# The four column groups' products of the modulation and the square sums, ordered one right behind another

## Chip, core and metric

The kernel runs on one core of a Trainium2 chip. The metric is device time in microseconds of one execution; the times before are the median of three runs. Engines are named as in the profile: PE is TensorE's matmuls and PEld its weight loads, DVE is VectorE, ACT ScalarE, POOL GpSimdE, SP the engine whose queue issues most of the DMAs.

## The reference, cut to what matters

A two-layer backbone over 1024 latent tokens and 256 context tokens, model width 1024, all in fp32. For each layer the conditioning vectors of latent and context tokens give a shift, a scale and a gate of 1024 numbers each:

```
def modulation(cond, w, b):
    m = jax.nn.silu(cond) @ w + b
    return jnp.split(m, 3, axis=-1)

h_lat = rms_norm(x_lat, norm_g[i]) * (1.0 + sc_l[:, None, :]) + sh_l[:, None, :]
y_lat, y_ctx = even_mixer(...)   # i = 0: global and windowed attention, 8 heads each
y_lat, y_ctx = odd_mixer(...)    # i = 1: convolution branch and neighbourhood attention
x_lat = x_lat + g_l[:, None, :] * y_lat
```

The result is `rms_norm(x_lat, final_g)`. Each rms norm needs, for each token, the sum of 1024 squares.

## The kernel before

Activations lie transposed: 128 of the 1024 channels on the partitions, tokens along the free dimension, in pieces of 256, 512 and 512 tokens. Each projection is done as three matmuls of split numbers (`mm3`, L351 to L354), accumulated over eight channel blocks in one PSUM bank. Layer 0 weaves attention (scores L529 to L533, outputs L480 to L485, row maxima L643 to L663) with the projections (`pq` and `pg`) of the next head group; layer 1 does the same with its own projections and, later, the output projection (`po`).

Two small sums use TensorE differently. They have only few output rows, so they use a quarter of the array's columns each, and write to one of four groups of 32 partitions of the bank:

- The modulation (`mod_part`, L181). Half of one of the three vectors, 512 columns, is the sum of eight products: `csil`, the activated conditioning of one channel block, 32 columns wide, by a 128x512 block of `mod_w` (tiles `mw`, loaded by SP). Block `dk` goes to column group `dk % 4`, so that each group sums two blocks. There are 12 banks `pm` of eight products. The first four banks are made by `mod_half` (L204) at the start of the program, with two blocks to a load. The other eight are made by `mod_steps` (L215), with four blocks to a load, so two calls of `mod_part` to a bank. This generator is advanced by `tick` (L831), in the middle of projections. A copy on ScalarE (L234) and four matmuls with `msel` (`mod_out`, L187) then add the four groups up.
- The square sum (`sum4`, L282). Squares of four channel blocks, summed over partitions by a matmul with ones, one block to a column group. Four banks `pb` of two calls each: in the norm of layer 0 (`norm_x`), at the end of layer 0 (`final_proj(1)`), and twice in the final norm (`out1_end`, pieces 1 and 2). The matmul of the block computed last, `i = 3`, is recorded first, and the three others are held behind it by `tc.issue_after`.

The order on each engine is not the order of the code. The framework's scheduler lays the instructions out along a timeline of its own: among those that are ready it takes the one with the lower priority number, which is the place in the recording unless the kernel changes it. `later(n)` (L292) adds `n` to that number for what is recorded inside; `tick` uses `later(100)` for the modulation, so that its steps yield to the projections. `tc.issue_after(x)` keeps what is recorded inside behind instruction `x`. Each engine then runs its own list strictly in order, waiting on semaphores; SP's list is a queue of DMA issues, in which each load of a tile with a limited number of buffers waits until its buffer is free. Names with numbers, such as pm_1024, are single tiles of a family.

Of the kernel before, what the change touches and what calls it, by code (L numbers as in the profile page):

```python
# [89 lines left out]
def tile_kernel(ctx: ExitStack, tc: tile.TileContext, a, out):  # L90
    nc = tc.nc
    VE, SC, GP, PE, SY = nc.vector, nc.scalar, nc.gpsimd, nc.tensor, nc.sync
# [50 lines left out]
    csil = kvp.tile([P, DK, 32], F32, tag="csil", name="csil")  # L143
# [36 lines left out]

    def mod_part(pb, w, dks):  # L181

        for k, dk in enumerate(dks):
            q = dk % 4 * 32
            PE.matmul(pb[q : q + 32, :], csil[:, dk, :], w[:, k, :], start=(dk < 4), stop=(dk >= 4))

    def mod_out(tr, row, l, part, j):  # L187

# [15 lines left out]
    def mod_half(l, part, j):  # L204

        pb = bank("pp", nm("pm"))
        for d2 in range(4):
            w2 = mw_tile()
            mm0.append(SY.dma_start(w2, mod_src(l, part, j, 2 * d2, 2 * d2 + 2)))
            mod_part(pb, w2, (2 * d2, 2 * d2 + 1))  # L210
        row = a0.tile([P, 512], F32, tag="ost", name=nm("mrow"), bufs=2)
        SC.copy(row, pb)
        mod_out(bank("tr", nm("trm")), row, l, part, j)

    def mod_steps(pool, halves):  # L215

        def load(l, part, j):
            ws = []
            for d in (0, 4):
                w = pool.tile([P, 4, 512], F32, tag="mw", name=nm("mw"), bufs=2)  # L220
                SY.dma_start(w, mod_src(l, part, j, d, d + 4))
                ws.append(w)
            return ws

        ws = load(*halves[0])
        for n_, hf in enumerate(halves):
            for _ in range(4):
                yield
            tag = "ov" if solo[0] else "tr"
            pb = bank(tag, nm("pm"))  # L230
            for d, w in enumerate(ws):
                mod_part(pb, w, range(4 * d, 4 * d + 4))
            row = pool.tile([P, 640], F32, tag="rt2", name=nm("mrow"), bufs=2)[:, :512]
            SC.copy(row, pb)  # L234
            yield
            yield
            mod_out(bank("ov" if solo[0] else "tr", nm("trm")), row, *hf)
            if n_ + 1 < len(halves):
                ws = load(*halves[n_ + 1])
            for _ in range(3):  # L240
                yield
# [40 lines left out]
    def sum4(pb, sqs, n, q):  # L282

        with ExitStack() as cx:
            for i in (3, 0, 1, 2):
                m = PE.matmul(pb[32 * i : 32 * i + 32, :n], one[:, 0:1].broadcast_to([P, 32]), sqs[i][:, :n],
                              start=(q == 0), stop=(q == 1))
                if i == 3:
                    cx.enter_context(tc.issue_after(m.ins))

    @contextmanager
    def later(n):  # L292

        p = tc.cur_priority
        tc.cur_priority = p + n
        yield
        tc.cur_priority -= n
# [418 lines left out]
    with ExitStack() as p0x:  # L716
# [6 lines left out]
        with tc.tile_pool(name="st0", bufs=1, reuse_waits="tile") as st0:  # L723
# [19 lines left out]
            def norm_x(c):  # L743
                n = CHUNKS[c][1]
                if c == 1:
                    pb = bank("st", nm("pb"))
                    for q in range(2):
                        sqs = []
                        for i in range(4):
                            j = 4 * q + i  # L750
                            if j < 6:
                                sq = kvp.tile([P, 512], F32, tag=("QH", "QL")[j % 2], name=nm("sq"), bufs=3)
                            else:
                                sq = a0.tile([P, 512], F32, tag="ost", name=nm("sq"), bufs=2)
                            SC.activation(sq[:, :n], xraw[c][4 * q + i], AF.Square)
                            sqs.append(sq)
                        sum4(pb, sqs, n, q)
                    acc = kvp.tile([P, 512], F32, tag="QH", name=nm("acc"), bufs=3)
                    acts0.append(SC.copy(acc[:, :n], pb[:, :n]))
                    return acc  # L760
# [223 lines left out]
    with tc.tile_pool(name="o0", bufs=1, reuse_waits="tile") as op_:  # L984
# [49 lines left out]
        def final_proj(c):  # L1034
# [9 lines left out]
            for e in range(DK):  # L1044
                yield from out0(final, e, c, *ws[e // 2])
                if c > 0:
                    SY.dma_start(X1[:, e, t0 - 256 : t0 - 256 + n], x1[c][:, e, :])
                if c == 1:
                    sqs.append(op_.tile([P, 512], F32, tag="sq1" if e % 4 < 3 else "acc1", name=nm("sq1"), bufs=3 if e % 4 < 3 else 1))
                    SC.activation(sqs[-1], x1[c][:, e, :], AF.Square)  # L1050
                    if e == 0:
                        pb = bank("tr", nm("pb"))
                    if e % 4 == 3:
                        sum4(pb, sqs[-4:], n, e // 4)
                    if e == 7:
                        accs[c].append(acc1())
                        SC.copy(accs[c][0], pb)
                elif e < na:
                    SC.activation(accs[c][e], x1[c][:, e, :], AF.Square)
                else:  # L1060
                    if c < 2:
                        sq = op_.tile([P, 512], F32, tag="sq1", name=nm("sq1"), bufs=3)
                    else:
                        sq = kvp.tile([P, 512], F32, tag="QL", name=nm("sq1"), bufs=3)
                    SC.activation(sq[:, :n], x1[c][:, e, :], AF.Square)
                    k = e % na if e < 7 else 0
                    (GP if (k if c == 2 else e % 2) else VE).tensor_tensor(accs[c][k], accs[c][k], sq[:, :n], op=ALU.add)
# [44 lines left out]
    with ExitStack() as l1x:  # L1112
# [407 lines left out]
        def out1_end(k):  # L1520
# [4 lines left out]
            for e in range(DK):  # L1525
                if k == 0:
                    if e % 2 == 0:
                        w = load_w(wp, a["od_wo"], e // 2, 256, WB, dks=range(4, 8))
                    yield from out1((4, 5, 6, 7), e, hf, *w, o, n)
                else:  # L1530
                    yield from out1((7,), e, hf, *wend[e // 2], o, n)
                x = x2[hf][:, e, o : o + n]
                if k:
                    sq = dlow.tile([P, 512], F32, tag=("ph", "pl")[e % 2], name=nm("sq2"), bufs=LOOK1 + 1)[:, :n]
                else:
                    sq = half("sq2", "hf") if e in SQ else pair("sqt", 512, "vT")[:, 0].bitcast(F32)
                SC.activation(sq, x, AF.Square)
                if k:
                    accs.append(sq)
                    if e % 4 == 3:  # L1540
                        sum4(pb, accs[-4:], n, e // 4)
                elif e in SQ:
                    accs.append(sq)
                else:
                    (GP if e in SQP[k] else VE).tensor_tensor(accs[e % 2], accs[e % 2], sq, op=ALU.add)
                yield
# [188 lines left out]
```

## Time and profile before

| | us |
|---|---|
| median of 3 runs | 1530.31 (1528.89 to 1530.62) |
| span of the profiled execution, first to last instruction | 1528.5 |
| TensorE busy in it | 1451.0 |
| the modulation's products (L185), 192 records, PE busy | 43.8 |
| the square sums' products (L286), 64 records, PE busy | 8.3 (5.3 at 512 columns, 3.0 at 256) |

The profiled execution's own time is known by its span alone. Each fp32 product of the two sums shows as two records, each projection matmul as one. A matmul's length in the profile contains its run through the array, so consecutive ones overlap; what one costs TensorE is read from the distance of starts. Stretches are given in us from the span's start: the modulation and first norm up to about 36 us, layer 0's attention woven with projections to about 900, layer 1's convolution to about 1180, its attention to about 1500, then the final norm.

### The profile page before, as it was taken

Reading aid. Unit: us, or ns where it says so; the run is one execution under the profiler, and the core shown is the slowest. Engines: PE = TensorE matmul, PEld = TensorE weight load, DVE = VectorE, ACT = ScalarE, POOL = GpSimd, SP = SyncE. Lnnn points to the kernel's source line nnn. Section 1 sums busy time; section 2 is a strip of 40 time slices with the busy share of each in tenths; the row PEclk is TensorE's granted clock in tenths of the full one; section 3 lists DMA queues with packets and bytes.
Section 4 is the critical chain, followed back from the end, with each engine's and each line's share of the span. In section 5 each row is a group of like instructions: output and inputs, shape, how many; then the busy total and the mean of one; then the engine's idle time right before and its main releaser. Section 6 shows DMA issues by size and latency. Waiting matters only on the chain.

```text
span 1528.5 us, 21545 instructions
## 1 busy us (share of the span) xinstructions
PE 1451.0 (95%) x7144; PEld 1167.2 (76%) x7144; DVE 1031.7 (67%) x2095; ACT 748.1 (49%) x1418; POOL 788.0 (52%) x628
## 2 busy tenths in 40 slices
PE   6999999998998999999999889999999999989996
PEld 2786877896896777886777568888887788868775
DVE  2643566589578856457676948899848666567766
ACT  3642433443435564447646665343334455455564
POOL 3360443555454766557645665665532434364665
PEclk9999999999999999999999999999999999989998
DMA  9564325422312246121202021210484677877642
GB/s 366 201 225 135 106 69 174 135 77 88 114 56 76 85 138 210 49 69 54 59 28 66 35 67 56 62 56 28 158 253 144 207 219 240 248 222 234 178 129 110
DMA packets 154167, 199.83 MB, mean 131 GB/s; under 512 B 14716, under 2 KB 95816, under 8 KB 154056
## 3 DMA queue, kind: packets, MB, share of 16 engines
q1 hardware_dynamic: 147392, 186.88, 38.9%
q10 hardware_dynamic: 6664, 11.57, 2.3%
q8 instruction: 56, 0.92, 0.3%
q14 instruction: 55, 0.45, 0.1%
HBM read 148.07 MB, written 49.02 MB: 129 GB/s over the span
## 4 chain that ended last, share of the span: by engine, by line
PE 79%; DVE 11%; issue 3%; DMA 3%; ACT 2%; POOL 1%; ACTq 0%; SPq 0%; DVEq 0%; POOLq 0%
PE p L352 6%; PE p L354 6%; PE p L353 6%; PE ov L480 5%; PE ov L482 4%; PE ov L481 4%; PE po L352 4%; PE st L533 4%; PE st L529 4%; PE po L353 4%; PE po L354 4%; PE pq L352 4%; PE pq L353 3%; PE pq L354 3%; PE pg L352 2%
## 5 line engine op out<-in xcount | busy, mean ns | idle before, releaser
L334 POOL TENSOR_TENSOR pl<-pf,ph 128x512 fp32r<-128x512 f32 (+4 forms) x321 | 394.0, 1239 | 384.9 <-ACT ph L331 337.3
L541 ACT ACTIVATE pf<-st 128x512 f32<-128x512 f32 x284 | 166.5, 597 | 203.6 <-PE st L533 165.2
L334 POOL TENSOR_TENSOR wl<-wr,wh 128x512 fp32r<-128x512 f32 (+2 forms) x131 | 169.3, 1302 | 136.5 <-ACT wh L331 124.0
L331 ACT CAST ph<-pf 128x512 fp32r<-128x512 f32 (+4 forms) x364 | 209.5, 588 | 27.1 <-PE ov L481 15.9
L352 PE MATMUL p<-hh,wh 128*128 128x512 f32 x448 | 176.0, 393 | 3.4 <-DVE spq L1233 1.3
L353 PE MATMUL p<-hl,wh 128*128 128x512 f32 x448 | 174.5, 390 | 0.0
L354 PE MATMUL p<-hh,wl 128*128 128x512 f32 x448 | 173.0, 391 | 0.0
L480 PE MATMUL ov<-ph,Vt 128*128 128x512 f32 (+4 forms) x364 | 141.0, 387 | 4.2 <-DVE y L693 2.0
L529 PE MATMUL st<-QH,KAt 128*128 128x512 f32 (+4 forms) x364 | 140.2, 386 | 3.9 <-ACT pf L541 3.1
L482 PE MATMUL ov<-pl,Vt 128*128 128x512 f32 (+4 forms) x364 | 141.1, 388 | 2.2 <-POOL pl L334 2.1
L481 PE MATMUL ov<-ph,Vt 128*64 128x512 f32 (+4 forms) x364 | 138.9, 381 | 0.0
L533 PE MATMUL st<-QL,KBt 68*128 68x512 f32 (+4 forms) x364 | 136.4, 386 | 0.9 <-issue 0.8
L1177 DVE SCALAR_TENSOR_TENSOR cps<-U,taps,cps 128x512 f32<-128x512 f32 x184 | 125.9, 748 | 0.7
L331 ACT CAST wh<-wr 128x512 fp32r<-128x512 f32 (+2 forms) x134 | 80.9, 613 | 84.1 <-PE po L353 15.9
L352 PEld LDWEIGHTS p<-hh,wh 128*128 128x128 f32 x448 | 84.2, 188 | 21.5 <-ACT spq L1231 1.6
L656 DVE TENSOR_REDUCE mp<-mx 128x1 f32<-128x512 f32 x128 | 85.3, 681 | 19.3 <-PE mx L655 18.3
L354 PEld LDWEIGHTS p<-hh,wl 128*128 128x128 f32 x448 | 84.1, 188 | 17.4
L353 PEld LDWEIGHTS p<-hl,wh 128*128 128x128 f32 x448 | 84.2, 188 | 17.1 <-issue 0.2
L1020 DVE SCALAR_TENSOR_TENSOR x<-po,modT,x 128x512 f32<-128x512 f32 (+1 forms) x72 | 46.9, 657 | 64.0 <-PE po L354 63.5
L352 PE MATMUL pq<-wh,hh 128*128 128x384 f32 x256 | 88.2, 344 | 1.0 <-ACT hh L331 1.0
L353 PE MATMUL pq<-wl,hh 128*128 128x384 f32 x256 | 87.3, 341 | 0.0
L354 PE MATMUL pq<-wh,hl 128*128 128x384 f32 x256 | 86.6, 342 | 0.0
(287 smaller groups left out, 3417.2 us busy)
## 6 DMA issues: line engine op xcount, KB each, us to landing
mw<-in_mod_w_dram SPq DMA_DIRECT2D x16, 1024.0 KB, 5.3
Q<-qs SPq DMA_DIRECT2D x40, 256.0 KB, 2.1
QH<-Q SPq DMA_DIRECT2D x80, 128.0 KB, 2.7
mw<-in_mod_w_dram SPq DMA_DIRECT2D x16, 512.0 KB, 6.8
wr<-in_od_d_dram SPq DMA_DIRECT2D x32, 256.0 KB, 3.1
wr<-in_ev_qkv_dram SPq DMA_DIRECT2D x16, 384.0 KB, 5.0
KAt<-KD SPq DMA_DIRECT2D x16, 384.0 KB, 6.5
wr<-in_od_wo_dram SPq DMA_DIRECT2D x22, 256.0 KB, 3.4
```

The source lines that it names most:

```text
L331: acts.append(SC.copy(hi, src))
L334: (GP if leng == "g" else VE).tensor_tensor(lo, src, hi.bitcast(F32), op=ALU.subtract)
L352: PE.matmul(o, lh, rh, start=first, stop=False)
L353: PE.matmul(o, lh, rl, start=False, stop=False)
L354: last.append(PE.matmul(o, ll, rh, start=False, stop=end))
L480: PE.matmul(o, V[:, 64:192], ph[:, :n], start=(t == 0), stop=False)
L481: PE.matmul(g.ov[0:64, q0 : q0 + n], V[:, 0:64], ph[:, :n], start=False, stop=False)
L482: PE.matmul(o, V[:, 64:192], pl[:, :n], start=False, stop=(last and g.sink is None))
L529: sts.append(PE.matmul(st[:, :n], KA[:, cs], g.QH[:, q0 : q0 + n], start=True, stop=False))
L533: PE.matmul(st[:, :n], KB[0:68, cs], g.QL[0:68, q0 : q0 + n], start=False, stop=True)
L541: acts.append(SC.activation(pf[:, :n], st[:, :n], AF.Exp, scale=1.0 if g.bias else SCALE))
L1177: VE.scalar_tensor_tensor(pc, uc, w, pc, op0=ALU.mult, op1=ALU.add)
```

## The change

```
@@ mod_part
-        for k, dk in enumerate(dks):
-            q = dk % 4 * 32
-            PE.matmul(pb[q : q + 32, :], csil[:, dk, :], w[:, k, :], start=(dk < 4), stop=(dk >= 4))
+        with ExitStack() as cx:
+            for k, dk in enumerate(dks):
+                q = dk % 4 * 32
+                m = PE.matmul(pb[q : q + 32, :], csil[:, dk, :], w[:, k, :], start=(dk < 4), stop=(dk >= 4))
+                if k == 0:
+                    cx.enter_context(tc.issue_after(m.ins))
+                    cx.enter_context(later(-100000))
@@ sum4
         with ExitStack() as cx:
             for i in (3, 0, 1, 2):
+                if i == 0:
+                    cx.enter_context(later(-100000))
                 m = PE.matmul(pb[32 * i : 32 * i + 32, :n], one[:, 0:1].broadcast_to([P, 32]), sqs[i][:, :n],
                               start=(q == 0), stop=(q == 1))
```

The first product of a call keeps its place in the schedule. The others of the call are held behind it and get a priority number that is lower than any other's, so that the scheduler takes them as soon as they are ready. No instruction is added or removed on any engine. The new lines shift line numbers: L185 becomes L186, L286 becomes L292, and the lines behind move down by 4 (between the two places) or 6.

The first place at which the order differs is TensorE's list in the middle of a gate projection of layer 0 (pg_1127; products of bank pm_1024), about 112 us into the span. Before, from one projection matmul to the next:

```order
L352 MATMUL pg_1127<-hh_174,gh_996 128x512
L185 MATMUL pm_1024<-mw_908,csil 32x512
L353 MATMUL pg_1127<-hl_175,gh_996 128x512
L185 MATMUL pm_1024<-mw_908,csil 32x512
L354 MATMUL pg_1127<-hh_174,gl_997 128x512
L185 MATMUL pm_1024<-mw_908,csil 32x512
L352 MATMUL pg_1127<-hh_174,gh_996 128x512
L185 MATMUL pm_1024<-mw_908,csil 32x512
L932 MATMUL trk_1058<-ident,pc_803 128x128 x3
L353 MATMUL pg_1127<-hl_175,gh_996 128x512
L185 MATMUL pm_1024<-mw_910,csil 32x512
```

Of the change, the same place:

```order
L358 MATMUL pg_1127<-hh_174,gh_996 128x512
L186 MATMUL pm_1024<-mw_908,csil 32x512 x4
L359 MATMUL pg_1127<-hl_175,gh_996 128x512
L360 MATMUL pg_1127<-hh_174,gl_997 128x512
L358 MATMUL pg_1127<-hh_174,gh_996 128x512
L938 MATMUL trk_1058<-ident,pc_803 128x128 x3
L359 MATMUL pg_1127<-hl_175,gh_996 128x512
L186 MATMUL pm_1024<-mw_910,csil 32x512 x4
```

The eight products, each between two projection matmuls, became two groups of four; the rest kept its order. Banks pm_2020 (four and four single ones), pm_3143 (five, two, one) and pm_3959 (one, seven) become two groups of four, one of eight and one of eight in the same way, and the square sum of `final_proj(1)` (one, three, four) two of four. The other modulation banks stood in groups already. Behind pm_2020 the scheduler's timeline runs differently, and instructions of all engines swap places with neighbours, in three stretches: up to about 480 us, about 840 to 960 us, and about 1200 to 1440 us.

The second place is SP's queue in layer 1's attention, where the keys (KAt), queries (QH, QL) and bias tiles (bm, bs) of a coming head are loaded, with weights (wr), about 1340 us into the span. Before:

```order
L1372 DMA bm_13525<-in_d_bm_dram 128x320
L371 DMA wr_14391<-in_od_wo_dram 128x512
L1382 DMA bs_13775<-in_d_bs_dram 128x320
L409 DMA KAt_11673<-KD_9582 64x1536
L410 DMA KAt_11673<-KD_9582 64x1536
L1361 DMA QH_13741<-QD_9578 64x512
L1362 DMA QH_13741<-QD_9578 64x512
L1363 DMA QL_13742<-QD_9578 64x512
L1372 DMA bm_13769<-in_d_bm_dram 128x440
```

Of the change:

```order
L377 DMA wr_14391<-in_od_wo_dram 128x512
L1388 DMA bs_13775<-in_d_bs_dram 128x320
L1378 DMA bm_13769<-in_d_bm_dram 128x440
L415 DMA KAt_11673<-KD_9582 64x1536
L416 DMA KAt_11673<-KD_9582 64x1536
L1367 DMA QH_13741<-QD_9578 64x512
L1368 DMA QH_13741<-QD_9578 64x512
L1369 DMA QL_13742<-QD_9578 64x512
```

The bias load bm_13769 moved from behind the keys and queries to ahead of them. At the head before it, the bias load bm_13274 moved the other way, from ahead of KAt_11670 to behind QL_13219.

The third place is the end of TensorE's list, with the last square sum (pb_15683), the transposing matmuls of the piece before it (trs_15672) and the broadcasts (bc). Before:

```order
L354 MATMUL po_3828_15737<-od_3247_13697,wl_15601 128x256
L267 MATMUL trs_15672<-ones,row_15670 128x2 x2
L286 MATMUL pb_15683<-sq_3821_15710,one 32x256
L286 MATMUL pb_15683<-sq_3815_15689,one 32x256
L286 MATMUL pb_15683<-sq_3817_15696,one 32x256
L286 MATMUL pb_15683<-sq_3819_15703,one 32x256
L286 MATMUL pb_15683<-sq_3829_15742,one 32x256
```

Of the change:

```order
L360 MATMUL po_3828_15737<-od_3247_13697,wl_15601 128x256
L292 MATMUL pb_15683<-sq_3821_15710,one 32x256
L292 MATMUL pb_15683<-sq_3815_15689,one 32x256
L292 MATMUL pb_15683<-sq_3817_15696,one 32x256
L292 MATMUL pb_15683<-sq_3819_15703,one 32x256
L271 MATMUL trs_15672<-ones,row_15670 128x2 x2
L292 MATMUL pb_15683<-sq_3829_15742,one 32x256
```

The first four products moved ahead of the transposing matmuls.

## The prediction

> **What bounds the kernel now.** I read the page from the top: the span, the engine totals, the granted clock, then who ends the chain.
>
> ```profile
> span 1528.5 us, 21545 instructions
> PE 1451.0 (95%) x7144; PEld 1167.2 (76%) x7144; DVE 1031.7 (67%) x2095; ACT 748.1 (49%) x1418; POOL 788.0 (52%) x628
> PEclk9999999999999999999999999999999999989998
> PE 79%; DVE 11%; issue 3%; DMA 3%; ACT 2%; POOL 1%; ACTq 0%; SPq 0%; DVEq 0%; POOLq 0%
> ```
>
> TensorE is busy for 95% of the span, the chain that ended last runs over it for 79%, and its clock is granted in full nearly everywhere. So a microsecond taken out of its queue is worth up to a microsecond, as long as nothing else is late. Next, the stretches in which the change moves instructions:
>
> ```profile
> core 0: us, PE busy (x) PEld busy (x) DVE busy (x) ACT busy (x) POOL busy (x), PEclk, DMA share, GB/s
> 120.00:160.00 40.00, 38.84 (x203) 29.36 (x203) 15.64 (x48) 10.72 (x24) 5.12 (x4) 1.00 0.50 172
> 200.00:330.00 130.00, 128.63 (x672) 105.86 (x671) 80.87 (x204) 52.40 (x114) 56.73 (x43) 1.00 0.37 119
> 330.00:500.00 170.00, 161.64 (x816) 135.07 (x815) 133.83 (x302) 74.22 (x156) 86.81 (x63) 0.97 0.26 82
> 840.00:960.00 120.00, 108.57 (x479) 80.61 (x478) 87.21 (x155) 74.43 (x139) 72.56 (x70) 0.93 0.17 57
> 1200.00:1440.00 240.00, 231.91 (x1174) 192.52 (x1175) 159.44 (x379) 130.68 (x257) 116.31 (x107) 0.98 0.78 226
> ```
>
> From 120 to 160 and from 200 to 330 us TensorE has next to no idle time, while VectorE, ScalarE and GpSimdE have a third to four fifths of theirs free: TensorE alone is the bound. From 330 to 500 VectorE is at 133.83 of 170 us (79%), from 840 to 960 TensorE loses 11 us to waits, from 1200 to 1440 the DMA engines are at 78%. In these three a saving may be partly eaten.
>
> **What one product costs alone.** The timeline of TensorE where one bank's eight modulation products stand one by one among a gate projection (a projection matmul is one record, a product two; columns are start, length, then the instruction):
>
> ```profile
> 112.02 0.39 PE L354 MATMUL pg<-hh,gl 128*128 128x512 f32 x1
> 112.25 0.39 PE L352 MATMUL pg<-hh,gh 128*128 128x512 f32 x1
> 112.57 1.05 PE L185 MATMUL pm<-mw,csil 128*32 128x512 f32 x2
> 113.55 0.49 PE L353 MATMUL pg<-hl,gh 128*128 128x512 f32 x1
> 113.97 1.05 PE L185 MATMUL pm<-mw,csil 128*32 128x512 f32 x2
> 114.95 0.49 PE L354 MATMUL pg<-hh,gl 128*128 128x512 f32 x1
> ```
>
> Projections follow each other every 0.23 us (112.02 to 112.25). With one product between them it is 1.40 (113.55 to 114.95). So a product alone costs 1.40 - 0.23 = 1.17 us.
>
> **What a run costs.** First four products side by side, then eight:
>
> ```profile
> 68.02 0.34 PE L353 MATMUL pq<-wl,hh 128*128 128x384 f32 x1
> 68.29 1.06 PE L185 MATMUL pm<-mw,csil 128*32 128x512 f32 x8
> 69.29 0.44 PE L354 MATMUL pq<-wh,hl 128*128 128x384 f32 x1
> 69.57 0.49 PE L932 MATMUL trk<-ident,pc 128*128 128x128 f32 x3
> ...
> 143.91 0.40 PE L354 MATMUL pg<-hh,gl 128*128 128x512 f32 x1
> 144.23 1.92 PE L185 MATMUL pm<-mw,csil 128*32 128x512 f32 x16
> 146.09 0.44 PE L663 MATMUL mx<-KAt,QH 128*128 128x384 f32 x1
> 146.37 0.27 PE L457 MATMUL trn<-ident,nmt 128*12 128x128 f32 x1
> ```
>
> Four: 69.57 - 68.02 = 1.55 for the run and two 384-wide matmuls. Such a one is shorter than the 512-wide one's 0.23; at the ratio of their widths 0.17 (an estimate), which leaves 1.55 - 0.34 = 1.21 us. The four column groups together take what one takes alone: 1.06 against 1.05 in length. Eight: 2.46 - 0.23 - 0.17 = 2.06 us. So what counts is how often TensorE is interrupted, not how many products there are.
>
> On this the Trainium skill speaks against the change. The weight loads of the products, min, median and longest in ns:
>
> ```profile
> L185 PEld LDWEIGHTS pm<-mw,csil x192: 106/109/156, 8.6 to 356.2; 128*32 128x32 f32 x192
> ```
>
> Its page "TensorE: Matmul & The Clock Gate", Part 3, "The mechanism", says that a weight load overlaps a running matmul only where the row groups differ, and all four products here use all rows. By that rule, three further pairs of weight loads at the median of 109 ns would make a run of four 0.65 us dearer (6 x 0.109), some 1.86. The trace disagrees: 1.06 for four. I keep the row.
>
> **The change part by part.** The order shows that the instructions are the same; on every engine only their places change. Of the sixteen banks summed this way ten keep the shape they had, most because the scheduler already had them in fours or eights, or because modulation loads come two products at a time in the first 40 us. Six change.
>
> (1) Bank pm_1024, near 112 us: eight interruptions become two runs of four. 8 x 1.17 - 2 x 1.21 = **6.9 us**. Until here nothing else on any engine is moved, and after it TensorE stays the bound (38.84 of 40 us), with DMA at half share: kept in full.
>
> (2) Bank pm_2020 and (3) bank pm_3143, near 211 and 275 us:
>
> ```profile
> 211.41 1.07 PE L185 MATMUL pm<-mw,csil 128*32 128x512 f32 x8
> 212.78 1.05 PE L185 MATMUL pm<-mw,csil 128*32 128x512 f32 x2
> ...
> 275.16 1.90 PE L185 MATMUL pm<-mw,csil 128*32 128x512 f32 x10
> 278.06 1.05 PE L185 MATMUL pm<-mw,csil 128*32 128x512 f32 x4
> 279.42 1.05 PE L185 MATMUL pm<-mw,csil 128*32 128x512 f32 x2
> ```
>
> pm_2020 is a run of four and four single ones (the first shown): 1.21 + 4 x 1.17 = 5.9, afterwards two runs of four, 2.4: **3.5 us**. pm_3143 is runs of five, two and one. A run of five lasts as long as eight (1.90 against 1.92), one of two as long as one: 2.06 + 1.21 + 1.17 = 4.4, afterwards one run of eight, 2.06: **2.4 us**. Both lie where TensorE is 99% busy.
>
> (4) Bank pm_3959, near 351 us, a single one and seven, becomes eight: 1.17 us of TensorE time.
>
> ```profile
> 351.58 1.02 PE L185 MATMUL pm<-mw,csil 128*32 128x512 f32 x2 [0.86 <-issue]
> 354.71 0.28 PE L457 MATMUL trn<-ident,nmt 128*12 128x128 f32 x1 [1.32 <-DVE nmt L446]
> ```
>
> TensorE waits before it and 3 us later for VectorE, so the time freed is likely to become longer waiting. Between 0 and 1.17 I take **0**.
>
> (5) The square sum near 841 us: one, three, four becomes four, four.
>
> ```profile
> 841.31 1.04 PE L286 MATMUL pb<-sq,one 128*32 128x512 f32 x2
> 843.19 1.06 PE L286 MATMUL pb<-sq,one 128*32 128x512 f32 x6
> ```
>
> Lengths as above, so one interruption of 1.17 goes. In the stretch that follows TensorE waits a tenth of its time for others. Half of it: **0.6 us**, bounds 0 and 1.17.
>
> (6) The last square sum is split: four of its products now stand ahead of the transposing matmuls of the piece before it, with which the final norm's chain begins.
>
> ```profile
> 1515.47 0.50 PE L267 MATMUL trs<-ones,row 128*128 128x2 f32 x4
> 1515.90 1.83 PE L286 MATMUL pb<-sq,one 128*32 128x256 f32 x16
> ```
>
> Its cost lies between nothing and half of 1.83 us, since the products can hide the wait for their last squares; it is near the tail, nothing covers it: **-0.5 us**.
>
> (7) The new order elsewhere: 600-odd rows of TensorE in the stretches 211 to 480, 840 to 960 and 1200 to 1440 us swap places with neighbours, and with them loads on SP's queue. The dearest wait in the last of these stretches, and one issue on the queue ahead of it:
>
> ```profile
> 1350.82 0.77 PE L1405 MATMUL mx<-KAt,QH 128*128 128x256 f32 x2 [2.56 <-DMA QH<-QD]
> ...
> 1339.69 0.46 SPq L1372 DMA_DIRECT2D bm<-in_d_bm_dram  x1
> ...
> 1340.00:1350.00 10.00, 7.31 (x30) 4.93 (x28) 4.29 (x12) 6.80 (x15) 6.66 (x6) 0.84 1.04 280
> 1350.00:1360.00 10.00, 9.18 (x31) 7.58 (x32) 8.28 (x17) 3.95 (x9) 6.85 (x7) 0.66 0.71 182
> ```
>
> The order moves one bias load ahead of the KAt and QH loads of just this wait: QH is issued 0.46 us later if the bias tile's buffer is free, **-0.5 us**. A whole wait like this costs 2.56 us and, by the granted clock, 1.6 and 3.4 us of pace in the two tens: 7.6 us. For the other swaps the trace has no price; bounds are one such wait gained or lost, and I take 0, since neighbours trade places in both directions.
>
> Sum: 6.9 + 3.5 + 2.4 + 0 + 0.6 - 0.5 - 0.5 = **12.4 us**. The profiled execution's span of 1528.5 would become 1516.1. The median, 1530.31, lies 1.8 above that span; I carry this over: **1517.9 us**.
>
> **The rivals.** *One wait more or less.* The swaps add one wait of 7.6 us in the three stretches (1525.5), or dissolve the one at 1350 (1510.3). For it: DMA is at 78% to 104% there, and a queue in order delays all behind it. Against more than one: the instructions and bytes are the same.
>
> *Absorbed by VectorE.* If VectorE set the pace from 330 to 500 us, terms 1 to 3 would end as waiting there, and about nothing stay: 1530.7. Against it: VectorE has 36 us free in this stretch, three times the gain, and its work arrives earlier by as much.
>
> *Slower, by SP's queue in the last stretch.* Bias loads that now stand ahead of KAt and QH wait for a buffer, and hold these back at several head changes. Two such waits more give 1533.1, three give 1540.7; it decides from the second on, 15.2 against 12.4. Against it: the other reordered KAt group near it has its bias load moved behind QH instead.
>
> *Loads in line.* If the six loads that follow in a run of four took their 109 ns each, one after another, a run would cost 0.65 us more. Terms 1 and 2 end with four such runs where one stood: 3 x 0.65 = 2.0 us less, 1519.9. The 1.06 us of the run of four speaks against it. The Trainium skill's rule above would give this.
>
> **How the numbers follow.** My forecast has 54%, a wait dissolved 16%, a wait more 14%, loads in line 1%: faster in all of these, 85%. Absorbed 5% and two waits more 5% are within 0.2%, about 3 us and about what a measurement of this kernel can tell from no change: 10%. Three waits more: 5%, slower. The range takes in the forecast with its bounds (0 and 1.17 in terms 4 and 5) and a wait either way: 1508 to 1526.
>
> **What would show it.** Right: products as x8 or x16 rows only, no x2 rows after 40 us, at 1.06 and 1.92; the first row of the attention after 112 us some 7 us earlier, and 12 us earlier by 290. Wrong: a run of four that lasts longer than 1.1; the lead of 12 us at 330 gone by 500 (VectorE); or a lead that survives to 1200 and shrinks by 1440, with new waits for QH.

## The result, and the profile after

The changed kernel takes 1519.13 us (median of 4 runs, 1517.79 to 1521.38), the kernel before beside it 1530.46 us (4 runs, 1528.89 to 1533.85): ratio 0.9921, 95% interval [0.9899, 0.9944], so 12 us or 0.8% faster. Gains in us are given by the ratio, unless two times are subtracted; the difference of two medians (here 11.3) can lie one or two us beside it. Two further sets of runs gave 0.9930 [0.9903, 0.9957] and 0.9929 [0.9912, 0.9946]. The forecast was 1517.9 us.

The page of the changed kernel, its span, engine totals, granted clock and chain:

```profile
span 1516.0 us, 21539 instructions
PE 1437.9 (95%) x7144; PEld 1164.0 (77%) x7144; DVE 1036.0 (68%) x2095; ACT 747.6 (49%) x1418; POOL 788.7 (52%) x628
PEclk7999999999999999999999999999999999999998
PE 79%; DVE 11%; DMA 3%; issue 3%; POOL 2%; ACT 1%; SPq 0%; DVEq 0%; POOLq 0%; ACTq 0%
```

The same 7144 matmuls keep TensorE busy 13.1 us less (1451.0 before), its share stays at 95%: the span of 1516.0 follows the bound down. The stretches of the prediction, in the same columns as there:

```profile
120.00:160.00 40.00, 38.33 (x213) 31.48 (x212) 16.02 (x49) 12.12 (x27) 7.49 (x6) 1.00 0.48 165
200.00:330.00 130.00, 129.32 (x711) 111.44 (x710) 91.09 (x209) 54.43 (x119) 58.94 (x46) 1.00 0.37 121
330.00:500.00 170.00, 160.91 (x840) 134.71 (x839) 139.13 (x307) 79.17 (x164) 91.08 (x68) 0.99 0.28 86
840.00:960.00 120.00, 106.36 (x476) 81.41 (x475) 88.93 (x152) 72.89 (x134) 75.69 (x73) 0.96 0.17 55
1200.00:1440.00 240.00, 234.37 (x1181) 194.44 (x1180) 165.58 (x384) 130.34 (x260) 120.32 (x108) 0.99 0.77 227
```

From 200 to 330 us TensorE is as full as before and does 711 matmuls instead of 672. The bank pm_1024 in TensorE's timeline:

```profile
114.46 0.39 PE L360 MATMUL pg<-hh,gl 128*128 128x512 f32 x1
114.69 0.39 PE L358 MATMUL pg<-hh,gh 128*128 128x512 f32 x1
115.01 1.06 PE L186 MATMUL pm<-mw,csil 128*32 128x512 f32 x8
116.00 0.50 PE L359 MATMUL pg<-hl,gh 128*128 128x512 f32 x1
...
117.45 1.06 PE L186 MATMUL pm<-mw,csil 128*32 128x512 f32 x8
```

Where one product stood between two projections there are now four, in the same 1.06 us: from 114.69 to 116.00 is 1.31 us, less a projection's 0.23 leaves 1.08 (1.21 was the price taken for a run of four). The other banks that changed, and the square sum near 841 us:

```profile
207.70 1.06 PE L186 MATMUL pm<-mw,csil 128*32 128x512 f32 x8
...
209.07 1.06 PE L186 MATMUL pm<-mw,csil 128*32 128x512 f32 x8
...
267.41 1.92 PE L186 MATMUL pm<-mw,csil 128*32 128x512 f32 x16
...
341.68 1.92 PE L186 MATMUL pm<-mw,csil 128*32 128x512 f32 x16 [0.21 <-issue]
...
829.54 1.06 PE L292 MATMUL pb<-sq,one 128*32 128x512 f32 x8
```

**The lead.** Since the work is the same in both, one can take the same matmul in two traces and subtract its starts. One such pair is the transposing matmul behind the bank pm_1274. Before it starts at 146.37 (its row is in the prediction), after at

```profile
142.67 0.27 PE L463 MATMUL trn<-ident,nmt 128*12 128x128 f32 x1
```

so the lead there is 3.70 us. The table has the median of such differences at several places, always against the first profile of the kernel before; the experiments' rows are used below (us, positive is earlier; the places are the times of before).

| profile | 107 | 125 | 137 | 200 | 221 | 252 | 289 | end |
|---|---|---|---|---|---|---|---|---|
| the changed kernel | -2.4 | 4.5 | 3.7 | 3.7 | 7.2 | 7.8 | 10.1 | 12.6 |
| the same, e4 | 0.2 | 7.1 | 3.3 | 1.8 | 5.3 | 5.9 | 8.2 | 4.4 |
| the same, e10 | -2.6 | 4.4 | 0.5 | 0.5 | 4.0 | 4.5 | 6.8 | 12.8 |
| modulation alone, e1 | -1.2 | 5.7 | 2.7 | 1.1 | 4.6 | 5.2 | 7.5 | 6.6 |
| one bank alone, e3 | 0.5 | 7.5 | 3.0 | 3.1 | 3.1 | 3.0 | 3.0 | -1.5 |
| changed, stores on ScalarE's queue, e6 | 0.3 | 7.3 | 7.3 | 7.3 | 10.9 | 11.7 | 14.0 | 14.2 |
| the kernel before again, e12 | -0.4 | -0.4 | -1.9 | -1.9 | -1.9 | -1.8 | -1.8 | -2.8 |

Up to 107 us all of these have the same order on TensorE, so the first column is chance: executions differ by up to 3 us in the first 60 us. From 107 to 125 the gain is 6.9 us in every kernel that has the bank in two runs: exactly term 1. From 200 to 221 it is 3.5 (term 2: 3.5), from 252 to 289 it is 2.3 (term 3: 2.4), in all that have those banks changed, and nothing in e3 and e12. But between 125 and 137 us a part of term 1 is lost again: 0.8 us in the first profile of the changed kernel, 3 to 4.4 in the others, except e6. The kernel before loses something there too, 1.5 us in e12.

The tail, with the last square sum in two halves:

```profile
1502.29 0.64 PE L292 MATMUL pb<-sq,one 128*32 128x256 f32 x8
1502.86 0.61 PE L271 MATMUL trs<-ones,row 128*128 128x2 f32 x4
1503.39 0.63 PE L292 MATMUL pb<-sq,one 128*32 128x256 f32 x6
1504.56 0.62 PE L292 MATMUL pb<-sq,one 128*32 128x256 f32 x2 [0.53 <-ACT sq L1543]
```

The second half waits 0.53 us for ScalarE's last square, and over the last 60 us the lead does not move (12.50 to 12.56). An effect below 1 us could not be seen here: the second profile of the kernel before gains 0.9 us on the first in this stretch (-3.7 to -2.8).

### The profile page after: what moved, and what is told of

It is laid out like the page before. It is cut to its first block, busy times and chain, and to the rows that moved or that the text cites. A ratio compares the mean times of both kernels' runs of the same rounds, so it can differ in the third digit from the quotient of the medians.

```text
span 1516.0 us, 21539 instructions
## 1 busy us (share of the span) xinstructions
PE 1437.9 (95%) x7144; PEld 1164.0 (77%) x7144; DVE 1036.0 (68%) x2095; ACT 747.6 (49%) x1418; POOL 788.7 (52%) x628
## 4 chain that ended last, share of the span: by engine, by line
PE 79%; DVE 11%; DMA 3%; issue 3%; POOL 2%; ACT 1%; SPq 0%; DVEq 0%; POOLq 0%; ACTq 0%
PE p L358 6%; PE p L360 6%; PE p L359 6%; PE ov L486 5%; PE ov L488 5%; PE ov L487 4%; PE po L358 4%; PE po L359 4%; PE po L360 4%; PE st L539 4%; PE st L535 4%; PE pq L358 3%; PE pq L359 3%; PE pq L360 3%; PE pg L358 2%
## 5 line engine op out<-in xcount | busy, mean ns | idle before, releaser
L337 ACT CAST ph<-pf 128x512 fp32r<-128x512 f32 (+4 forms) x364 | 209.5, 588 | 22.2 <-PE ov L487 12.6
L535 PEld LDWEIGHTS st<-QH,KAt 128*128 128x128 f32 x364 | 69.6, 191 | 24.9 <-ACT pf L547 9.9
L488 PEld LDWEIGHTS ov<-pl,Vt 128*128 128x128 f32 x364 | 69.9, 192 | 24.1 <-POOL pl L340 7.1
```

The lines of the kernel that those rows point to most:

```text
L337: acts.append(SC.copy(hi, src))
L488: PE.matmul(o, V[:, 64:192], pl[:, :n], start=False, stop=(last and g.sink is None))
L535: sts.append(PE.matmul(st[:, :n], KA[:, cs], g.QH[:, q0 : q0 + n], start=True, stop=False))
```

## The experiments

The theory at the start was that of the prediction: each interruption of TensorE's full-array matmuls by a column-group product costs 1.17 us, one run costs the same whether it has one product or four, and what is saved stays saved. The rival was that the scheduler's swaps of neighbours decide the rest, by several us either way.

**e1, the modulation alone.** Only the edit in `mod_part`.

> Only the modulation's products are run together (its edit alone; the square sums' code is as before). Theory (every interruption of TensorE by a product costs 1.17 us, a run of four 1.21, a run of eight 2.06, and TensorE is the bound): terms 1 to 4 of the prediction, 6.9 + 3.5 + 2.4 + 0 = 12.8 us, so about 12 us under the kernel before in the same job, within 0.15% of the changed kernel. Rival (the gain is the luck of neighbours swapped by the scheduler, one wait of 7.6 us more or less): the gain is anywhere between 4 and 20 us, and the lead does not stand at 7 us right behind the bank at 112 us.

Measured: 1522.56 us (8 runs, 1517.18 to 1527.34) against 1531.09, ratio 0.9938 [0.9912, 0.9964]: 9.5 us. It carries nearly all of the gain; the changed kernel in the same set has 10.7.

**e2, the square sums alone.** Only the edit in the square sums.

> Only the square sums' products are run together (the modulation's code is as before). Theory: one interruption of 1.17 us less near 841 us, up to half of it swallowed by later waits: 0.6 us (0 to 1.17) under the kernel before, which this job cannot tell from no change. Rival (swaps of neighbours decide): several us either way, as the order behind 841 us changes too.

Measured: 1532.14 us (12 runs), ratio 1.0000 [0.9980, 1.0021]. No change is seen; the theory's 0.6 us is below what this can tell, as was expected, and a change of several us is not there.

**e3, one bank alone.** The kernel before, with only the eighth bank run together:

```diff
     def mod_part(pb, w, dks):
+        if dks[0] == 0:
+            banks[0] += 1
...
+                if k == 0 and banks[0] == 8:
+                    cx.enter_context(tc.issue_after(m.ins))
+                    cx.enter_context(later(-100000))
```

> Only the bank at 112 us (pm_1024, eight products one by one) becomes two runs of four; all other modulation banks and the square sums' code are as before. Theory: the lead is 8 x 1.17 - 2 x 1.21 = 6.9 us right behind it, and stays so: 6 to 7.5 us under the kernel before, with about 3.5 and 2.4 us less lead than the changed kernel behind 211 and 275 us. Rival (swaps decide the rest): the lead at 130 us is 6.9, but at the end it is something else by 3 us or more.

Measured: 1529.13 us (12 runs), ratio 0.9983 [0.9964, 1.0003], 2.6 us, and the interval holds no change as well. A miss: the 6.9 us are there at 125 us, and 4.4 of them are gone at 137. So the price was right, and "stays saved" was wrong for this bank. The trace shows where it goes. First the kernel before, SP's queue (two modulation loads of 1 MB, then the store of a piece of the gate) and ScalarE:

```profile
117.85 0.38 SPq L221 DMA_DIRECT2D mw<-in_mod_w_dram  x1
123.75 0.38 SPq L221 DMA_DIRECT2D mw<-in_mod_w_dram  x1
125.11 0.33 SPq L875 DMA_DIRECT2D G<-sg  x1
...
130.85 0.60 ACT L389 ACTIVATE sg<-pg 128x512 f32<-128x512 f32 x1 [3.36 <-DMA G<-sg]
```

Then e3, the same with TensorE's row:

```profile
115.02 0.39 SPq L229 DMA_DIRECT2D mw<-in_mod_w_dram  x1
116.20 0.44 SPq L229 DMA_DIRECT2D mw<-in_mod_w_dram  x1
116.97 0.76 SPq L883 DMA_DIRECT2D G<-sg  x1
...
127.85 0.60 ACT L397 ACTIVATE sg<-pg 128x512 f32<-128x512 f32 x1 [7.81 <-DMA G<-sg]
...
129.22 0.50 PE L360 MATMUL pg<-hh,gh 128*128 128x512 f32 x1 [2.69 <-DVE sg L398]
```

A load may start when the bank has used up the buffer that it will fill. One by one, the products freed the two buffers 5.9 us apart; run together they free them 1.2 us apart, so 2 MB go onto the queue right ahead of the gate's store. The store of 128 KB then takes 10.9 us from issue to landing (116.97 to 127.85), where it took 5.7 before (125.11 to 130.85). The gate's tile `sg` has only two buffers, shared with the modulation's row (`tag="rt2"`, `bufs=2`): ScalarE has to wait for the landing, VectorE for ScalarE, and TensorE for VectorE, 2.69 us. Some 1.7 us more (an estimate, 0.17 of 10 us) go to the granted clock, 0.83 in e3 from 120 to 130 us. That part is not shown to come from the store: in the second profile of the kernel before (e12, the second of these rows) the clock is 0.86 from 130 to 140 us, and TensorE waits only 0.2 us for `sg`.

```profile
120.00:130.00 10.00, 6.81 (x35) 6.11 (x36) 3.84 (x15) 1.40 (x5) 0.00 (x0) 0.83 0.69 226
```

```profile
130.00:140.00 10.00, 10.00 (x54) 9.05 (x54) 4.53 (x16) 1.70 (x5) 0.00 (x0) 0.86 0.35 110
```

With the stores on SP's queue the store lands at 127 to 129 us in all the profiles of such an order, whenever it was issued, so who comes earlier tends to wait longer (4.9 us in e11, 2.7 in e3, 2.0 in e4). But this does not settle the loss. The first profile of the changed kernel and e10 are the same program and come here within 0.2 us of each other (-2.4 and -2.6), yet one loses 0.8 us and the other 3.9. In e10 the store lands 1.65 us later (128.84 against 127.19), TensorE waits for `sg` 2.2 us in all instead of 0.7, and the clock is 0.83 from 130 to 140 us.

**e4, the changed kernel beside its parts.**

> The changed kernel again, beside its parts on the same chip. Theory and rival alike: 10 to 12.5 us under the kernel before. It is the sum of its parts by the theory (the modulation alone 12, the square sums alone 0.6, less 0.5 at the tail); by the rival the parts need not add up.

Measured: 1520.24 us (7 runs), ratio 0.9930 [0.9903, 0.9957], 10.7 us. The parts agree with it: e3 gains 2.6 us and e1 another 6.9 (9.5 - 2.6), against 3.5 + 2.4 = 5.9 for terms 2 and 3. With intervals of 3 to 4 us to either side this is no proof.

**e5 to e7, the gates' stores on another queue.** To see whether it is the store that holds TensorE, the stores go onto ScalarE's queue in e3's kernel (e5), in the changed kernel (e6) and in the kernel before (e7):

```diff
-                mark[0] = SY.dma_start(Gs[u][:, m, t0 : t0 + n], sg[:, :n])
+                mark[0] = SC.dma_start(Gs[u][:, m, t0 : t0 + n], sg[:, :n])
```

> As e3_one_bank (only the bank at 112 us run together), but the gates' stores G<-sg of the first layer are issued on ScalarE's DMA queue instead of SyncE's, behind whose two modulation loads of 1 MB the 128 KB store took 10.9 us to land in e3. Theory (term 1 was cut at the store: the products that end together free both buffers, both loads go ahead of the store, and TensorE waits 2.8 us at a slowed clock for the tile): the store lands within 4 us of its issue, the wait for sg is under 0.8 us, and the lead at 136 us is 6 to 7 us instead of 2.5; in total 6 to 7 us under the kernel before, if the store's new place costs nothing elsewhere. Rival (the DMA engines are full, so a store on any queue lands when the loads are done, near 127 us): wait and lead stay as in e3, 2 to 3 us in total.

> The changed kernel with the gates' stores of the first layer issued on ScalarE's DMA queue. Theory: the 3 to 4 us that term 1 lost come back, some 13 to 15 us under the kernel before (1516 to 1518 where the changed kernel had 1519 to 1520). Rival (full DMA engines): as the changed kernel, 10 to 11 us.

> The kernel before with only the gates' stores of the first layer moved to ScalarE's DMA queue: the control. TensorE waited 0.2 us for sg there, so by both theories within 3 us of the kernel before.

At the place itself TensorE's wait goes, as the theory had it. The rows of e6, and TensorE's waits for `sg` from 105 to 140 us (in total, times, longest):

```profile
113.36 0.38 SPq L225 DMA_DIRECT2D mw<-in_mod_w_dram  x1
115.87 0.39 SPq L225 DMA_DIRECT2D mw<-in_mod_w_dram  x1
...
117.17 0.34 ACTq L881 DMA_DIRECT2D G<-sg  x1
...
123.51 0.60 ACT L395 ACTIVATE sg<-pg 128x512 f32<-128x512 f32 x1 [3.27 <-DMA G<-sg]
```

```profile
PE pg L358 <- DVE sg L396: 0.2, 1, 0.2
```

e4 is the right one to compare, since there too the start-up was on time. Its second load, its store, on SP's queue, and ScalarE:

```profile
115.99 1.25 SPq L225 DMA_DIRECT2D mw<-in_mod_w_dram  x1
117.34 1.19 SPq L881 DMA_DIRECT2D G<-sg  x1
...
127.55 0.60 ACT L395 ACTIVATE sg<-pg 128x512 f32<-128x512 f32 x1 [7.19 <-DMA G<-sg]
```

There the store lands after 10.2 us (117.34 to 127.55), in e6 after 6.3 (117.17 to 123.51). TensorE waits 0.2 us where e3, e4 and e10 wait 2.0 to 2.7 at once, the clock is 1.00 from 120 to 130 us where e4 has 0.83, and the lead at 137 us is 7.3: term 1 is kept whole. But the queue makes only a part of the 3.9 us. By the packets in the traces, the middle one of the store's 128 packets starts 5.7 us after the issue in e4 and 4.5 in e6, the last one 9.8 and 5.7: most of the difference is a slow tail of e4's store, for which no cause was found. The first profile of the changed kernel (5.5 and 6.8) has hardly any of it.

e5 started 2.4 us late and keeps 6.2 us of term 1 (-2.4 to 3.8), as the first profile of the changed kernel, equally late, keeps 6.1 on SP's queue. Its control e7 started 2.6 us late, with the stores on the same queue, so these two can be compared as well: e5's lead over e7 is 7.1 us at 125 us and 6.3 from 137 to 325. e3's lead over the kernel before, on SP's queue and counted from 107 us, fell from 6.9 to 2.5; 1.7 of that may be the clock's. e5's store landed after 7.2 us, where 4 were expected.

The Trainium skill, page "DMA: Bandwidth & Descriptors", section "Issuing engines are not separate DMA queues", says that DMAs started by different engines run on the same 16 DMA engines and that this saves only the sequencer's time. The traces do not decide on it. In e6 the store's first packet starts 0.9 us sooner after the issue than in e4 (3.6 against 4.5), and the issue itself is 0.85 us shorter (0.34 against 1.19), as the page would have it; between e5 and e10, with the store 3.1 us behind the first load in both, it is 1.8 us (3.9 against 5.8) at an issue 0.6 us shorter (0.34 against 0.93), one profile each.

The times in all are another matter. e6: 1518.28 us, ratio 0.9919 [0.9896, 0.9942], 12.4 us, between the 13 to 15 of the theory and the 10 to 11 of its rival, so that it decides nothing; e5: 1531.53 us, 0.9995 [0.9978, 1.0012], with 6 to 7 us expected, a miss; and the control e7, which was to be neutral, is 8.6 us slower (1539.68 us), 1.0056 [1.0037, 1.0075]. The other queue also changed the order behind this place, on TensorE and VectorE among others, and e7 falls back by 4.9 us between 325 and 410 us and by 3 to 4 between 855 and 940. Against their control, e5 gains 8.2 us and e6 21.4. The first fits term 1 kept whole (6.9); the second is more than any term accounts for, and why e7's order is so poor was not settled.

**e8, one column group for all.** The eight products of a modulation bank go to column group 0, and the sum that the four groups needed is left to the accumulation there:

```diff
-                q = dk % 4 * 32
-                m = PE.matmul(pb[q : q + 32, :], csil[:, dk, :], w[:, k, :], start=(dk < 4), stop=(dk >= 4))
+                m = PE.matmul(pb[0:32, :], csil[:, dk, :], w[:, k, :], start=(dk == 0), stop=(dk == 7))
```

> The changed kernel, but all eight products of a modulation bank go to column group 0 (rows 0 to 31 of the bank), accumulating there, and the copy and the product that gathers the row use 32 partitions; the square sums keep four groups. The result is the same sum in another order. Theory (a run of four costs what one costs because the four column groups run at once): a run in one group takes 0.86 us a product (the second four of a run of eight add 1.92 - 1.06 = 0.86 to the first), so four take some 3.6 and eight some 7.1 us instead of 1.06 and 1.92; eight banks behind 40 us become about 5 us dearer each, 35 to 45 us slower than the changed kernel. Rival (the cost is that of the interruption, whatever the group): a run of four stays at 1.1 to 1.6 us and the time within 5 us of the changed kernel.

A run of four and a run of eight of e8:

```profile
140.62 3.62 PE L185 MATMUL pm<-mw,csil 128*32 128x512 f32 x8
...
167.02 7.05 PE L185 MATMUL pm<-mw,csil 128*32 128x512 f32 x16
```

3.62 and 7.05 us, as expected (3.6 and 7.1). So what makes a run cheap is not that TensorE is interrupted once; it is that the four column groups work at the same time, and a lone product leaves three of them idle. The prediction's "what counts is how often TensorE is interrupted" is only true of products in different groups. Four products more in one group add 3.43 us (7.05 - 3.62), 0.86 each; so of a lone product's 1.17 us only some 0.3 are the interruption (an estimate). The time, 1569.12 us, ratio 1.0253 [1.0229, 1.0277], is some 50 us above the changed kernel; 35 to 45 were expected for the eight later banks alone, and the lead of e8 is already -7.0 us between 30 and 60 us, by the first four banks, which had been left out.

**e9, another bank taken apart.** In the changed kernel the bank pm_1274, a run of eight in both, is ordered one by one:

```diff
-                mod_part(pb, w, range(4 * d, 4 * d + 4))
+                if n_ == 4:
+                    for k in range(4):
+                        mod_part(pb, w[:, k : k + 1, :], [4 * d + k])
+                        yield
+                else:
+                    mod_part(pb, w, range(4 * d, 4 * d + 4))
```

> The changed kernel with one other bank taken apart: pm_1274, near 140 us, a run of eight in both kernels (1.92 us), is ordered one product at a time among the projections; the banks behind it keep runs of four or eight. Theory (1.17 us for each interruption, 2.06 for a run of eight): 8 x 1.17 - 2.06 = 7.3 us of TensorE time more, so about 7 us slower than the changed kernel in the same job. Rival (lone products are cheap where nothing else is held up, and what was gained at 112 us was luck): within 2 us of the changed kernel.

Measured: 1535.20 us (12 runs, 1529.15 to 1540.60), 16.4 above the changed kernel in the same set (1518.80), 14.4 by the ratios (1.0023 [1.0003, 1.0042] against 0.9929). The direction is the theory's, the size is not. The `yield`s also pushed the later banks back, the last one by 60 us (343 to 403 us), and between 140 and 460 us the order differs so much that the starts of single matmuls no longer tell where time goes. Between 400 and 450 us e9's lead scatters about 4 to 8 where e10's is 8.7; from 480 us on e9 is 13.6 us behind e10. Neither the 7.3 nor what came on top of it can be read off, so this run is no clean price.

**e10, the changed kernel a third time.**

> The changed kernel in the same job, for comparison. 10 to 11 us under the kernel before; in its profile the wait for sg near 126 us ends at 127 to 129 us whatever the start-up took, so the lead at 136 us is 2.5 to 4 us and not the 6.9 of term 1.

Measured: 1518.80 us (6 runs), ratio 0.9929 [0.9912, 0.9946], 10.9 us. The bank gains 6.9 (-2.6 to 4.4), TensorE waits 2.03 us for `sg`, a clock of 0.83 from 130 to 140 us follows, and of term 1 are left 3.0 us (0.5 + 2.6). The lead itself is 0.5, not the 2.5 to 4 expected: a miss. The store landed at 128.84 as expected, but the late start-up and the clock come on top.

**e11, runs of eight.** Both calls of a bank in one run:

```diff
-            for d, w in enumerate(ws):
-                mod_part(pb, w, range(4 * d, 4 * d + 4))
+            mod_part(pb, ws, range(8))
```

> The changed kernel with both calls of a bank in one run: pm_1024 and pm_2020 become runs of eight (a run of eight is 2.06, two of four are 2.42). Theory: 0.36 us for pm_2020, nothing left of it for pm_1024, since TensorE waits at the gates' store until 127 to 129 us anyway and both modulation loads are now issued at once: within 1 us of the changed kernel, the lead at 136 us 2.5 to 4 us. Rival (the store is held up by no load): 0.7 us, with the lead at 136 us higher by as much.

Measured: 1525.64 us (10 runs, 1518.13 to 1528.17), ratio 0.9963 [0.9948, 0.9978]: 6.8 us slower than e10 by the medians, 5.2 by the ratios, a miss. The theory's mechanism did more than expected:

```profile
115.64 1.03 SPq L225 DMA_DIRECT2D mw<-in_mod_w_dram  x2
116.77 0.60 SPq L880 DMA_DIRECT2D G<-sg  x1
...
129.31 0.80 PE L357 MATMUL pg<-hh,gh 128*128 128x512 f32 x1 [4.94 <-DVE sg L395]
```

Both loads now start in one go, the store lands after 11.2 us, TensorE waits 4.94 us, and 1.4 us of term 1 are left (lead -0.3 to 1.1) instead of 3.0. The rest arises later: e11's profile is 0.7 us ahead of e10's at 300 us and 8.5 behind at the end. It was not traced.

**e12, the kernel before profiled again.**

> The kernel before, profiled a second time, nothing changed. If the loss at 1350 us (TensorE at 20.3 busy us and a granted clock of 0.80 between 1340 and 1365 us) belongs to its order of loads, it stands in this execution too, and the 3 to 5 us that the changed kernel has gained there are the change's; if it is chance of one execution, TensorE is busy 22 us or more there. In the bank at 112 us and the wait at the gates' store nothing can differ but by the start-up: the wait for sg stays at 0.2 us. Ratio 1 within 0.2%.

Ratio 0.9992 [0.9971, 1.0014]. TensorE's wait for `sg` is 0.2 us, as expected. The window around the dear wait near 1350 us, in the first profile of before, and in this one:

```profile
1340.00:1365.00 25.00, 20.31 (x80) 15.53 (x79) 17.48 (x42) 14.16 (x28) 14.78 (x13) 0.80 0.81 215
```

```profile
1340.00:1365.00 25.00, 20.59 (x88) 14.38 (x88) 18.64 (x44) 14.11 (x30) 17.31 (x16) 0.93 0.88 254
```

The wait for QH stands in both (2.6 and 2.0 us), and TensorE is busy as little in the second (20.59 us, where 22 or more would have meant chance), so the loss belongs to the order. But the clock around it is 0.80 in one and 0.93 in the other, and the second execution gains 2.8 us on the first between 1325 and 1460 us. Of the changed kernel, e4 and e10 in the same window:

```profile
1340.00:1365.00 25.00, 22.89 (x98) 18.71 (x99) 20.51 (x42) 15.90 (x31) 18.23 (x15) 0.86 0.80 225
```

```profile
1340.00:1365.00 25.00, 24.25 (x114) 18.91 (x114) 20.07 (x44) 15.20 (x29) 19.03 (x15) 1.00 0.75 211
```

The changed kernel gains 3.1, 3.4 and 4.7 us there in its three profiles, but 2.8 of it, as e12 shows, can be chance. The long wait for QH is gone in all three. In two a wait for KAt stands in its place, 2.2 and 2.0 us; in e10, the same program, neither is over 0.2. In e1 the wait for QH stands, with 3.3 us.

## Why the prediction was right, step by step

The time is 1.2 us off, well inside the range. That closeness is in part luck: the total hides one term that was too large, gains that were not foreseen, and a scatter that is larger than the smaller terms.

- **What bounds the kernel** held: busy time fell by 13.1 us and the span by 12.5.
- **A lone product at 1.17 us, a run of four at 1.21, of eight at 2.06:** the gains that follow from these prices held to 0.1 us, in five profiles at three banks. The Trainium skill's rule (page "TensorE: Matmul & The Clock Gate", Part 3, "The mechanism"), that a weight load overlaps only where row groups differ, would by the prediction's estimate have made a run of four cost 1.86 us. It costs 1.08 to 1.21; the 1.06 that the prediction set against the 1.86 is its length. The reason given, that it is the interruptions that count, fell with e8: it is the column groups' working at once. The Trainium skill's page "TensorE: Matmul & The Clock Gate", section "Why this matters for your kernels", has a figure on this side: 2.38 times for three such tiles. Here four take 1.06 us instead of 3.62, 3.4 times.
- **(1) pm_1024, 6.9 us, "kept in full":** the term that failed. 6.9 us were gained and 3.0, 3.1, 3.9 and 6.1 kept, in the four profiles with the modulation changed and the stores on SP's queue; 4.0 in the mean (against e12, which lost 1.5 at 130 us to a clock of 0.86, it would be 5.5). The waits for `sg` account for 0.7 to 2.2 us of the loss; in the three profiles that lost 3 to 3.9, a clock of 0.83 over 10 us, some 1.7 us (an estimate), accounts for most of the rest, and its cause is open. "DMA at half share" was read from a mean over 40 us. Within these it is 0.79 from 120 to 130 us and 0.05 from 140 to 150, and it was in the full part that two loads and a store met. The prediction looked at who had time free, not at what the products' end would set off: the two 1 MB loads.
- **(2) 3.5 and (3) 2.4:** 3.5 and 2.3 measured, in every profile. Another 0.5 us came between 221 and 252 us, not foreseen and not traced. Between 137 and 200 us e4 and e1 lost 1.5 and 1.6 us, where their clock is 0.83 and 0.86 from 140 to 150 us, and the two others nothing.
- **(4) 0, (5) 0.6, (6) -0.5, (7) -0.5:** none of them can be told from chance by itself. From 289 us to the end the four profiles gain 2.5, -3.7, 6.0 and -0.9 us, 0.9 in the mean, against -0.4 in the sum, and the unchanged kernel loses 0.9 on itself. Of (6) one can say that no cost is seen: the second half waits for its squares anyway. In (7) the sign was read from one bias load; what the runs show there is another wait in the place of the one for QH, or none. The square sums alone (e2) change nothing.
- **The sum:** 4.0 - 0.8 + 3.5 + 0.5 + 2.3 + 0.9 = 10.4 in the mean of the four profiles (0.8 is the loss between 137 and 200 us), against 12.4 forecast and 12.1, 10.7 and 10.9 measured in three sets. The lead of 12 us forecast by 290 us was 8.0 to 12.5, counted from 107 us. That the first profile ended 12.5 us ahead owes something to chance: it kept more of term 1 than the others and made up for a start-up 2.4 us late.
- **The rivals.** Not absorbed by VectorE: in the first profile the lead near 500 us (13.1) is above that near 325 (10.9), and in e4, e10 and e1 it is 8.1, 9.9 and 9.4 against 8.2, 6.8 and 7.5 at 289. No two waits more in the last stretch. Loads in line: refuted by the length of 1.06 us. What took a part of the gain, a wait for a transfer, was looked for at 1350 us and stood at 126.

## What to carry to other kernels

Small products in different column groups were worth being ordered side by side where they stood singly among full-array matmuls: four cost what one cost, and the saving can be read from two start-to-start times. When a run frees several buffers at once, look at the loads that this lets go and at what stands behind them on the same queue; a mean DMA share over 40 us did not show it here (0.50, with 0.79 in the ten that mattered). And before a term of a microsecond is weighed, profile the unchanged kernel twice: here the two kept step from 137 to 360 us, but drifted apart by 1 to 4 us in several stretches, 1.5 us near 130 among them.

## What the runs showed of the hardware

- A 128 KB store behind two 1 MB loads on one queue on the whole started the later, the closer it followed the first of them. From its issue to its first packet it took 7.8 us at a distance of 1.1 us (e11), 7.6 at 2.0 (e3), 5.6 at 2.9 (e1), 5.8 at 3.1 (e10), 4.5 to 4.8 at 3.8 to 3.9 (the changed kernel, e4 and e9), 3.0 at 7.3 (before). Its landing scatters more, since the last packets do: 11.2, 10.9, 9.5, 8.8, 7.2 to 10.2 and 5.7 us after the issue, in the same order.
- The same program, e4 and e10, took spans of 1524.1 and 1515.7 us. Their difference arises at no single place: e10 is 2.8 us behind at 107 us, then gains 1.5 near 146, 3.1 between 330 and 380, 3.8 near 730 and 3.3 between 1080 and 1360, and loses 0.9 between 560 and 720. The mean granted clock is 0.974 in both.
